# Where the tiles that TensorE reads start in on-chip memory: from 32, 128 or 224 bytes past a multiple of 256 to a multiple of 256

## The chip, the cores and the metric

One core of one Trainium2 chip runs the whole program, in one launch. The metric is the time of that core in microseconds of the device, smaller being better. Of three runs of the kernel before, the median is 2795.87 us (2795.35 to 2801.29).

## The reference

Two layers over 256 context tokens and 2048 latent tokens (a grid of 32 rows by 64 columns), width 1024, all in float32. Cut to what matters here:

```
# layer 0, convolution branch
a, b, z = split(h @ w_in, 3)                # 1024 x 3072
u = depthwise_conv31(a * sigmoid(b)) + dw_b
x = x + gate * ((silu(layer_norm(u)) * silu(z)) @ w_out)
# layer 1, attention branch
q, k, v, z = split(h @ w_in, 4)             # 1024 x 4096, 16 heads of 64
# latent tokens: 8 x 16 grid neighbours (with a bias) and all 512 cached context keys in one softmax
s = concat(q @ k_window + bias, q @ k_context)
p = softmax(s)
o = p_window @ v_window + p_context @ v_context
x = x + gate * ((o * silu(z)) @ w_out)
```

Ahead of each layer stands h = rms_norm(x) * (1 + scale) + shift, with shift, scale and gate from a small product with the conditioning vector; behind the last one stands a final rms_norm.

## The kernel before

Every large product is made of three: each operand is split into a rounded high part and the rest, and high x high, high x low and low x high are added up in one bank of the accumulation memory. The type of these operands is float32r (float32 data that TensorE reads in its reduced-precision form). TensorE issues 16081 matmuls, and nearly each has its own weight load, since the stationary operand changes with every instruction.

Two phases follow each other:

- `phase1`: the convolution layer (`conv_layer`, groups `ci_ps`, an order written out by hand with due times on TensorE, ScalarE, VectorE and GpSimd), its output product (`conv_out_pipeline` and `conv_out`, groups `co_p` and `co_s`), then the projections of the attention layer (`na_rest`, groups `ni_`; `na_values`, groups `v_ps`), with the mixing of context tokens (`pa_`, `po`) and the making of bias tables at their side.
- `phase2`: 64 heads and token groups of four units each. A unit computes scores in `sample_unit` (`sa_S`: 512 context columns and 352 to 480 window columns), softmax probabilities `p`, eight transposes through TensorE (`sa_T`, with the identity as the moving operand), and, for each pair of units, the product with the values (`sa_O`, 256 columns wide). `out_group` multiplies by the output weights (`o`, 512 wide). TensorE and VectorE follow the written order here.

In the projections (`project`) the moving operand is the activation block, 512 or 256 columns wide, and the stationary one the weight:

```
for k in ks:
    matmul(out, wh[:, k, :], hh[:, k, :], ...)   # stationary, moving
    matmul(out, wh[:, k, :], hl[:, k, :], ...)
    matmul(out, wl[:, k, :], hh[:, k, :], ...)
```

In `conv_out` it is the other way round: the normalised tokens (`yh`, `yl`) are stationary and the weight (`wh`, `wl`) moves.

On-chip memory is given out in pools, one behind the other from the left, and from the right end. A pool starts where the one before it ended, so sizes that are no multiple of 256 bytes shift all that follows. The program's own allocation (a matter of the code, no measurement) places the tiles that TensorE reads like this, in bytes of one partition:

| tiles | pool | start past a multiple of 256 |
|---|---|---|
| identity, all-ones | `consts` (left) | 128 |
| split weights (`wh`, `wl` of `ci`, `ni`, `wv`), normalised tokens (`ln_s_yh`, `ln_s_yl`) | `sp`, tag `t4` (left) | 32 |
| output weights `w2`, tokens `y` of `out_group`, context keys and values of the last five of each eight heads | `ap` (left) | 32 |
| activation blocks `h_s_hi`, `h_s_lo`, output weights `co_h`, `co_l` | `slots` (left, behind `sm`) | 224 |
| `h_p_hl`, `h_s_hl`, `ln_y`, context tokens' tiles (`pa_`, `po_`) | right side and `hp` | 224 |
| queries, keys, values, probabilities `p`, `pt`, context keys and values of the first three of each eight heads | `ep`, `pt` (right) | 224 |

So in `ci`, `ni` and `co_s` the moving tile starts at 224 and the stationary one at 32; in `v_ps` it is the other way round (the weight moves, at 32). In `co_p`, `pa_`, `po` and `o` both start alike (224 and 224, or 32 and 32).

Of the kernel before, what the change touches and what calls it, by code (L numbers as in the profile page):

```python
# [11 lines left out]
F32 = mybir.dt.float32  # L12
# [6 lines left out]
P = 128  # L19
# [56 lines left out]
class Kern:  # L76
    def __init__(self, ctx, tc, io):
        self.tc, self.nc, self.io = tc, tc.nc, io
        self.ctx = ctx
        self.more, self.more_bufs, self.turn = None, 0, 0  # L80
        self.tail = False
        self.s0, self.begun = None, []
        self.cp = ctx.enter_context(tc.tile_pool(name="consts", bufs=1))
        self.dr = ctx.enter_context(tc.tile_pool(name="scratch", bufs=1, space=bass.MemoryType.DRAM))
        d = lambda name, shape: self.dr.tile(shape, F32, name=name, tag=name)
        self.zc_d = d("zc_d", [D, NTOK])
        self.wl_d = d("wl_d", [3 * NK, P, D])
        self.vc_d = d("vc_d", [2, D, VCOLS // 2])
        self.x1_d = d("x1_d", [NTOK, D])
        self.qh_d = d("qh_d", [D, NTOK])  # L90
        self.ql_d = d("ql_d", [D, NTOK])
        self.ks_d = d("ks_d", [NH, 2, DH, NTOK])
        self.vp_d = d("vp_d", [NPR, NH, 2, DH])
        self.vs_d = d("vs_d", [GW // CW, NSA // GW, CW, NH, 2, DH])
        self.bm_d = d("bm_d", [NH, 3, P, 3, 480])
        self.zn_d = d("zn_d", [D, NTOK])
        self.kc_d = d("kc_d", [NH, 2, DH, NCTX])
        self.cvs_d = d("cvs_d", [NCTX, NH, 2, DH])
        self.w2_d = d("w2_d", [2, D, D])
        self.x2_d = d("x2_d", [NTOK, D])  # L100
        self.gate_d = d("gate_d", [2, 2, D])
        self.rpb_d = d("rpb_d", [P + 1, RPB_PITCH])
        self.yp_d = d("yp_d", [NK, 2, P, NPR])
# [32 lines left out]
        return t0 if src == "p" else NPR + t0  # L136


    def constants(self):
        nc, cp, io = self.nc, self.cp, self.io  # L140
        self.ident = cp.tile([P, P], F32, tag="ident", name="ident")
        make_identity(nc, self.ident)
        self.ones = cp.tile([P, P], F32, tag="ones", name="ones")
        nc.vector.memset(self.ones, 1.0 / D)
        self.mhalf = cp.tile([P, 1], F32, tag="mhalf", name="mhalf")
        nc.vector.memset(self.mhalf, -0.5)

        c = self.vectors("cond", [io["c_ctx"], io["c"][0]], lambda rows: nc.scalar.activation(rows, rows, AF.Silu))()
        self.cs = cp.tile([P, NK, 32], F32, tag="cs", name="cs")
        nc.vector.memset(self.cs, 0.0)  # L150
        nc.vector.tensor_copy(self.cs[:, :, 0:2], c.rearrange("p g k -> p k g"))
        self.sel = cp.tile([P, 2], F32, tag="sel", name="sel")
        nc.vector.tensor_reduce(out=self.sel, in_=self.ident.rearrange("p (j x) -> p x j", x=32)[:, 0:2], axis=AX.X, op=ALU.add)
# [1218 lines left out]
    def phase1(self):  # L1372
        tc = self.tc
        with ExitStack() as c:
            late = c.enter_context(ExitStack())
            self.rp = late.enter_context(tc.tile_pool(name="rp", bufs=1, side="right"))
            self.sp = Tagged(c.enter_context(tc.tile_pool(name="sp", bufs=1)), {"slot": 4, "t4": 8, "raw": 2, "st": 6})
            self.sm = c.enter_context(tc.tile_pool(name="sm", bufs=3))
            self.sp.apart["slot"] = c.enter_context(tc.tile_pool(name="slots", bufs=1))
            self.ps = c.enter_context(tc.tile_pool(name="ps", bufs=2, space=bass.MemoryType.PSUM))  # L1380
            with tc.tile_pool(name="convp", bufs=2) as self.up, tc.tile_pool(name="acc", bufs=2, space=bass.MemoryType.PSUM) as self.pc:
# [28 lines left out]
            with tc.tile_pool(name="bp", bufs=1, side="right") as self.bp:  # L1410
                with tc.tile_pool(name="mb", bufs=1, side="right") as self.mb, tc.tile_pool(name="more", bufs=1, space=bass.MemoryType.PSUM) as self.more:
                    self.more_bufs = 4
                    side = itertools.chain(self.context_keys(), self.masked_bias())
# [5 lines left out]
                with tc.tile_pool(name="pq", bufs=2, side="right") as pq, tc.tile_pool(name="pqs", bufs=1, space=bass.MemoryType.PSUM) as pps:  # L1419
                    side = itertools.chain(self.gated_weights(), self.context_values())  # L1420
                    side = self.mixed(self.prompt_attention(pq, pps), side, 24 / 52)
# [6 lines left out]
            with tc.tile_pool(name="po", bufs=1, side="right") as po, tc.tile_pool(name="pops", bufs=1, space=bass.MemoryType.PSUM) as pps:  # L1428
                side = self.prompt_out(po, pps)
# [40 lines left out]
    def T(self, tag, shape, dt, name):  # L1470
        if tag in self.early:
            return self.ep.tile(shape, dt, tag=tag, name=name, bufs=self.early[tag])
        return self.sp.tile(shape, dt, tag=tag, name=name)

    def phase2(self):
        tc = self.tc
        with ExitStack() as c:
            bufs = {"w2": 4, "ckr": 8 - NEAR, "cvr": 8 - NEAR, "pt": 2, "st": 4, "y": 14, "x": 3, "row": 1}
            self.sp = Tagged(c.enter_context(tc.tile_pool(name="ap", bufs=1)), bufs)
            self.sm = c.enter_context(tc.tile_pool(name="asm", bufs=6))  # L1480
            self.ps = c.enter_context(tc.tile_pool(name="aps", bufs=1, space=bass.MemoryType.PSUM))
            self.fg = None

            self.sp.apart["pt"] = c.enter_context(tc.tile_pool(name="pt", bufs=1, side="right"))
            E = mybir.EngineType
            c.enter_context(tc.manual_schedule(engines={E.PE, E.DVE}))
            self.attention()
# [138 lines left out]
    def sample_unit(self, hd, j):  # L1626

        nc, T, h, b, G = self.nc, self.T, hd.h, hd.b, hd.G
        nm = f"sa{G}_{h}_{j}"
        R = KEY_ROWS[G][1]  # L1630
        nl = 32 * R
        cs = slice(j * P, j * P + P)
        S = self.bank("S", nm + "_S", 2, 1024)
        jj = j % 2
        ctx, loc = S[:, :512], S[:, 512 : 512 + nl]
        kw = hd.k[:, :, CW * JFIRST[j] : CW * JFIRST[j] + 32].rearrange("p r (a c) -> p a r c", c=CW)
        self.scores(ctx, hd.q[:, cs], hd.ql[:, cs], hd.ctx[h, 0])
        self.scores(loc, hd.q[:, cs], hd.ql[:, cs], kw)
        yield
        m = self.sm.tile([P, 8], F32, tag="m", name=nm + "_m")  # L1640
        nc.vector.tensor_reduce(out=m[:, 0:1], in_=ctx, axis=AX.X, op=ALU.min)  # L1641
        bm = hd.bm[:, JKIND[j], :nl]
        nc.vector.tensor_tensor_reduce(loc, loc, bm, 1.0, m[:, 0:1], ALU.add, ALU.min, accum_out=m[:, 2:3])  # L1643
        yield
        p = T("p", [P, 1024], F32, nm + "_p")
        n = slice(0, 512 + nl)
        nc.scalar.activation(p[:, n], S[:, n], AF.Exp, scale=-1.0, bias=m[:, 2:3], accum_out=m[:, 3:4])  # L1647
        nc.vector.reciprocal(m[:, 3:4], m[:, 3:4])  # L1648
        nc.gpsimd.tensor_scalar(out=p[:, n], in0=p[:, n], scalar1=m[:, 3:4], scalar2=1.0, op0=ALU.mult, op1=ALU.mult)  # L1649
        yield  # L1650
        ts = []
        for part, w, x in ((0, P, 0), (1, CW * R, 512)):
            t = self.bank("T", f"{nm}_T{part}", 2)
            for c in range(4):
                nc.tensor.transpose(t[:w, c * P : c * P + P], p[:, x + c * w : x + c * w + w], self.ident)  # L1655
            ts.append((part, w, t[:w].rearrange("p (c q) -> p c q", c=4)))
        yield
        if jj == 0:
            hd.pt[j // 2] = T("pt", [P, 2, 2, 4, 2, P], F32R, nm + "_pt")
        pt = hd.pt[j // 2]  # L1660
        for part, w, t in ts:

            at = 1 - jj if part == 0 else jj
            nc.scalar.copy(pt[:w, 0, part, :, at], t)  # L1664
            self.rest_dve(pt[:w, 1, part, :, at], t, pt[:w, 0, part, :, at])
# [263 lines left out]
```

## Time and profile before

| | |
|---|---|
| median of three runs | 2795.87 us |
| the profiled execution | 2797.14 us, its span 2795.4 us |
| TensorE busy | 2696.5 us, 96% of the span, 16081 matmuls |
| VectorE, ScalarE, GpSimd busy | 1767.9, 1377.2, 1404.0 us (63%, 49%, 50%) |
| clock granted to TensorE | 0.991 of full speed |
| moved to and from main memory | 533.86 MB, 191 GB/s over the span |

The busy time of TensorE is a sum over pipelined records whose ends are modelled: a 512-wide matmul is recorded with some 395 ns while the next one starts some 230 ns after it. What one costs is the time from its start to the next one's start, called its step from here on; it is read from the timeline, or, where all run back to back, from the record, which is longer than the step by a fixed amount.

### The profile page before, as it was taken

Reading aid. Unit: us, or ns where it says so; the run is one execution under the profiler, and the core shown is the slowest. Engines: PE = TensorE matmul, PEld = TensorE weight load, DVE = VectorE, ACT = ScalarE, POOL = GpSimd, SP = SyncE. Lnnn points to the kernel's source line nnn. Section 1 sums busy time; section 2 is a strip of 40 time slices with the busy share of each in tenths; the row PEclk is TensorE's granted clock in tenths of the full one; section 3 lists DMA queues with packets and bytes.
Section 4 is the critical chain, followed back from the end, with each engine's and each line's share of the span. In section 5 each row is a group of like instructions: output and inputs, shape, how many; then the busy total and the mean of one; then the engine's idle time right before and its main releaser. Section 6 shows DMA issues by size and latency. Waiting matters only on the chain. (4 is left out here: it accounts for less than half of the span.)

```text
span 2795.4 us, 45265 instructions
## 1 busy us (share of the span) xinstructions
PE 2696.5 (96%) x16081; PEld 2320.7 (83%) x16081; DVE 1767.9 (63%) x3052; ACT 1377.2 (49%) x2437; POOL 1404.0 (50%) x1589
## 2 busy tenths in 40 slices
PE   6999999999999999999999999989999999999998
PEld 4888877776777889899998888878888898888887
DVE  4678778878985610013546533368787787878885
ACT  4446454456453322134222244257676676666774
POOL 4686776557554343345223335245455555555563
PEclk9999999999999999999999999999999999999999
DMA  7233554455645554446889986598666767956652
GB/s 258 68 122 121 177 192 123 167 190 193 191 113 164 164 168 129 133 127 193 262 285 330 365 267 183 185 248 229 203 198 197 203 170 204 279 176 202 194 165 100
DMA packets 443833, 533.86 MB, mean 191 GB/s; under 512 B 77745, under 2 KB 320393, under 8 KB 443480
## 3 DMA queue, kind: packets, MB, share of 16 engines
q1 hardware_dynamic: 435568, 503.82, 59.5%
q10 hardware_dynamic: 6664, 22.82, 2.1%
q0 software_dynamic: 1376, 4.33, 0.4%
q8 instruction: 128, 2.10, 0.3%
q14 instruction: 97, 0.79, 0.1%
HBM read 355.14 MB, written 179.79 MB: 191 GB/s over the span
## 5 line engine op out<-in xcount | busy, mean ns | idle before, releaser
L1649 POOL TENSOR_SCALAR sa_p<-sa_p,sa_m 128x992 f32<-128x992 f32 (+2 forms) x256 | 277.6, 1084 | 420.2 <-DVE sa_m L1648 290.0
L514 POOL TENSOR_TENSOR cv_p<-cv_p,cv_p 128x640 f32<-128x640 f32 (+1 forms) x240 | 359.1, 1496 | 123.1 <-ACT cv_p L511 110.1
L1664 ACT CAST sa_pt<-sa_T 128x512 fp32r<-128x512 f32 (+3 forms) x512 | 274.9, 588 | 200.3 <-PE sa_T L1655 195.4
L113 DVE TENSOR_TENSOR sa_pt<-sa_T,sa_pt 128x512 fp32r<-128x512 f32 (+3 forms) x512 | 328.2, 682 | 3.2 <-ACT sa_pt L1664 3.1
L362 PE MATMUL ci_ps<-h_s_hi,ci_wh 128*128 128x512 f32 x768 | 310.7, 405 | 8.2 <-ACT z L481 3.2
L363 PE MATMUL ci_ps<-h_s_lo,ci_wh 128*128 128x512 f32 x768 | 306.8, 399 | 0.0
L364 PE MATMUL ci_ps<-h_s_hi,ci_wl 128*128 128x512 f32 x768 | 306.6, 399 | 0.0
L1647 ACT ACTIVATE sa_p<-sa_S,sa_m 128x992 f32<-128x992 f32 (+2 forms) x256 | 267.0, 1043 | 64.3 <-DVE sa_m L1643 56.5
L1655 PE MATMUL sa_T<-ident,sa_p 128*128 128x128 f32 (+3 forms) x2048 | 271.7, 275 | 9.3 <-DVE sa_pt L113 9.1
L1655 PEld LDWEIGHTS sa_T<-ident,sa_p 128*128 128x128 f32 (+3 forms) x2048 | 236.9, 137 | 46.9 <-issue 14.8
L1641 DVE TENSOR_REDUCE sa_m<-sa_S 128x1 f32<-128x512 f32 x256 | 176.2, 688 | 145.3 <-PE sa_S L1623 134.0
L511 ACT ACTIVATE cv_p<-u,ws 128x640 f32<-128x640 f32 (+1 forms) x256 | 190.8, 777 | 133.8 <-DVE u L478 100.2
L534 DVE SCALAR_TENSOR_TENSOR cv<-u,dw,cv 128x640 f32<-128x640 f32 (+1 forms) x240 | 195.9, 816 | 0.5
L1684 PE MATMUL sa_O<-sa_pt,a_v 120*128 120x256 f32 (+5 forms) x1280 | 191.1, 280 | 0.0
L362 PEld LDWEIGHTS ci_ps<-h_s_hi,ci_wh 128*128 128x128 f32 x768 | 146.3, 191 | 49.9 <-ACT z L481 6.4
L534 DVE SCALAR_TENSOR_TENSOR cv<-cv_d,dw,cv 128x640 f32<-128x640 f32 (+1 forms) x224 | 182.6, 815 | 0.0
L1643 DVE CUSTOM_DVE_ANT_0 sa_S<-sa_S,a_bm,sa_m 128x480 f32<-128x480 f32 (+2 forms) x256 | 170.9, 668 | 13.6 <-DMA a_bm<-bm_d 4.7
L1679 PE MATMUL sa_O<-sa_pt,cv 128*128 128x256 f32 x1024 | 174.8, 293 | 4.7 <-ACT sa_pt L1664 1.1
L364 PEld LDWEIGHTS ci_ps<-h_s_hi,ci_wl 128*128 128x128 f32 x768 | 146.3, 190 | 35.5
L363 PEld LDWEIGHTS ci_ps<-h_s_lo,ci_wh 128*128 128x128 f32 x768 | 146.4, 191 | 32.8
L1684 PEld LDWEIGHTS sa_O<-sa_pt,a_v 120*128 120x128 f32 (+2 forms) x1280 | 166.8, 191 | 0.0
L362 PE MATMUL ni_s<-h_s_hi,nis_wh 128*128 128x512 f32 x384 | 152.6, 397 | 2.3 <-ACT ni_s_f L1047 2.1
(808 smaller groups left out, 7128.8 us busy)
## 6 DMA issues: line engine op xcount, KB each, us to landing
adaw<-in_ada_w SPq DMA_DIRECT2D x24, 1024.0 KB
ci_w<-in_conv_w_in SPq DMA_DIRECT2D x48, 512.0 KB
a_bm<-bm_d SPq DMA_DIRECT2D x32, 720.0 KB
x_s<-in_x_sample SPq DMA_DIRECT2D x32, 512.0 KB
vs_d<-v_s SPq DMA_DIRECT2D x128, 128.0 KB
a_qh<-qh_d SPq DMA_DIRECT2D x128, 128.0 KB
a_ql<-ql_d SPq DMA_DIRECT2D x128, 128.0 KB
a_v<-vs_d SPq DMA_DIRECT2D x32, 480.0 KB
```

The lines of the kernel that those rows point to most:

```text
L113: self.nc.vector.tensor_tensor(out=lo, in0=src, in1=hi.bitcast(F32), op=ALU.subtract)
L362: self.nc.tensor.matmul(out, wh[:, k, :], hh[:, k, :], start=k == 0, stop=False)
L363: self.nc.tensor.matmul(out, wh[:, k, :], hl[:, k, :], start=False, stop=False)
L364: self.nc.tensor.matmul(out, wl[:, k, :], hh[:, k, :], start=False, stop=k == NK - 1)
L511: nc.scalar.activation(t, st["u"][:, 0, j : j + nh], AF.Copy, scale=self.ws[:, ct, j : j + 1])
L514: nc.gpsimd.tensor_tensor(out=st["t", 0], in0=st["t", 0], in1=st["t", j], op=ALU.add)
L534: nc.vector.scalar_tensor_tensor(out=st["acc", b], in0=d, scalar=w, in1=st["acc", b], op0=ALU.mult, op1=ALU.add)
L1647: nc.scalar.activation(p[:, n], S[:, n], AF.Exp, scale=-1.0, bias=m[:, 2:3], accum_out=m[:, 3:4])
L1649: nc.gpsimd.tensor_scalar(out=p[:, n], in0=p[:, n], scalar1=m[:, 3:4], scalar2=1.0, op0=ALU.mult, op1=ALU.mult)
L1655: nc.tensor.transpose(t[:w, c * P : c * P + P], p[:, x + c * w : x + c * w + w], self.ident)
L1664: nc.scalar.copy(pt[:w, 0, part, :, at], t)
L1684: nc.tensor.matmul(dst, v[:w, c0 + c].rearrange("p s d -> p (s d)"), loc[:, lo:hi], start=False, stop=s == 1 and c == 3)
```

## The change

Four paddings are allocated and never touched: 128 bytes ahead of the constants, 224 bytes at the right edge, 96 bytes in a pool of its own behind the constants, and 192 bytes in `sm`. The pool `sm` has three buffers to a tag, so there it is 576 bytes. A fifth, of 128 bytes, stands in `ep` for phase 2. The all-ones tile (512 bytes) moves from the constants into `sm`, which ends with phase 1; it is used only in `norm_stages`. The probabilities `p` become 992 columns wide in place of 1024, which is all that they use (512 + 480); with three buffers, `ep` shrinks by 384 bytes for it and grows by the 128 of padding.

By these sizes all behind the constants on the left moves by 128 - 512 + 96 = -288 bytes (32 past becomes 0), `slots` and what stands behind `sm` by a further 576 + 512 (224 becomes 0), and the right side by -224 (224 becomes 0). No instruction that computes or moves data is added or removed.

```diff
         self.cp = ctx.enter_context(tc.tile_pool(name="consts", bufs=1))
+
+        self.pad(self.cp, 128)
+        self.pad(ctx.enter_context(tc.tile_pool(name="edge", bufs=1, side="right")), 224)
+        self.pad(ctx.enter_context(tc.tile_pool(name="gap", bufs=1)), 96)
...
+    def pad(self, pool, n):
+        pool.tile([P, n // 4], F32, tag="pad", name="pad")
+
     def constants(self):
...
-        self.ones = cp.tile([P, P], F32, tag="ones", name="ones")
+        self.ones = self.sm.tile([P, P], F32, tag="ones", name="ones", bufs=1)
...
             self.sm = c.enter_context(tc.tile_pool(name="sm", bufs=3))
+            self.pad(self.sm, 192)
...
             self.fg = None
+            self.pad(self.ep, 128)
...
-        p = T("p", [P, 1024], F32, nm + "_p")
+        p = T("p", [P, 992], F32, nm + "_p")
```

## The prediction

> **What bounds the kernel now.** I read the page first (busy time, slices), then who made TensorE wait, then busy times by stretch, then TensorE's timeline.
>
> ```profile
> PE 2696.5 (96%) x16081; PEld 2320.7 (83%) x16081; DVE 1767.9 (63%) x3052; ACT 1377.2 (49%) x2437; POOL 1404.0 (50%) x1589
> PEclk9999999999999999999999999999999999999999
> PE ada_ps L227 <- DMA adaw<-in_ada_w: 11.7, 3, 10.8
> PE sa_T L1655 <- DVE sa_pt L113: 9.1, 18, 1.1
> 500.00:720.00 220.00, 212.21 (x958) 161.56 (x957) 184.92 (x248) 123.38 (x183) 138.31 (x113) 0.98 0.55 180
> 2100.00:2400.00 300.00, 296.32 (x2009) 268.32 (x2008) 236.53 (x532) 202.98 (x377) 159.65 (x235) 1.00 0.72 199
> ```
>
> TensorE is busy 96% of the span at full clock, and its two largest waits are 11.7 and 9.1 us in total. In the stretches (length, then busy us of TensorE, its weight loads, VectorE, ScalarE, GpSimd) the next engine, VectorE, has 184.92 of 220 us and 236.53 of 300. So the time is the sum of TensorE's steps (from one matmul's start to the next one's), and the change can act through the step alone. The timeline (start, length of the record, line) gives it; rows between the first and the last of a run are left out:
>
> ```profile
> 300.17 0.40 PE L363 MATMUL ci_ps<-h_s_lo,ci_wh 128*128 128x512 f32 x1
> ...
> 303.90 0.40 PE L364 MATMUL ci_ps<-h_s_hi,ci_wl 128*128 128x512 f32 x1
> ...
> 800.79 0.39 PE L857 MATMUL co_s<-co_h,ln_s_yh 128*128 128x512 f32 x1
> ...
> 801.72 1.09 PE L860 MATMUL co_s<-co_h,ln_s_yl 128*128 128x512 f32 x4
> ...
> 724.67 0.39 PE L857 MATMUL co_p<-co_h,ln_y 128*128 128x512 f32 x1
> ...
> 726.94 0.39 PE L857 MATMUL co_p<-co_h,ln_y 128*128 128x512 f32 x1
> ...
> 2103.13 0.39 PE L1785 MATMUL o<-w2l,1_1_y0h 128*128 128x512 f32 x1
> ...
> 2104.03 0.39 PE L1786 MATMUL o<-w2h,1_1_y0l 128*128 128x512 f32 x1
> ```
>
> All four are 512 columns wide. `ci` makes 16 steps in 303.90 - 300.17 = 3.73 us: 0.233 us each. `co_s` makes 4 in 0.93 us: 0.233. `co_p` makes 10 in 2.27 us: 0.227. `o` makes 4 in 0.90 us: 0.225 to 0.227. `co_s` and `co_p` run the same code lines with the same moving weight; only the stationary tile lies elsewhere. By the allocation, moving and stationary tiles start 224 and 32 bytes past a multiple of 256 in `ci` and `co_s`, but alike in `co_p` (224, 224) and `o` (32, 32). So placing costs something: 6 to 7 ns where the two differ. No row shows a 512-wide step with both at 0.
>
> The 256-wide matmuls:
>
> ```profile
> 1101.07 0.28 PE L362 MATMUL ni_s<-h_s_hl,nip_wh 128*128 128x256 f32 x1
> ...
> 1102.89 0.28 PE L363 MATMUL ni_s<-h_s_hl,nip_wh 128*128 128x256 f32 x1
> ...
> 1334.78 0.28 PE L1011 MATMUL v_ps_s<-wv_s_wh,h_s_lo 128*128 128x256 f32 x1
> ...
> 1335.84 0.28 PE L1011 MATMUL v_ps_s<-wv_s_wh,h_s_lo 128*128 128x256 f32 x1
> ...
> L364 PE MATMUL ni_p<-h_p_hl,nip_wl 128*128 128x256 f32 x192 | 53.2, 277 | 0.0
> L1333 PE MATMUL pa_O<-pa_pt,pa_v x64: 277/283/285, 1663.9 to 1743.8; 128*128 128x256 f32 x64
> ```
>
> `ni` makes 16 steps in 1.82 us (0.114), `v_ps` 9 in 1.06 (0.118); both have tiles that differ (224 and 32, 32 and 224). A 256-wide record is 0.163 us longer than its step (277 against 114 in `ni`), so the median of `pa_O`, 283 ns, is a step of 0.120, with tiles that start alike. At this width equal placing gains nothing by the rows, and may cost.
>
> **The change part by part.** First the sum's main term. The 512-wide matmuls whose two tiles differ now:
>
> ```profile
> L362 PE MATMUL ci_ps<-h_s_hi,ci_wh 128*128 128x512 f32 x768 | 310.7, 405 | 8.2 <-ACT z L481 3.2 <-DVE adao L239 2.3 <-ACT u L476 1.7
> L362 PE MATMUL ni_s<-h_s_hi,nis_wh 128*128 128x512 f32 x384 | 152.6, 397 | 2.3 <-ACT ni_s_f L1047 2.1
> L362 PE MATMUL ni_s<-h_s_hi,nip_wh 128*128 128x512 f32 x192 | 76.4, 398 | 0.0
> L819 PE MATMUL co_s<-co_h,ln_s_yh 128*128 128x512 f32 x160 | 65.5, 409 | 0.8 <-POOL ln_s_yh L107 0.8
> L858 PE MATMUL co_s<-co_l,ln_s_yh 128*128 128x512 f32 x96 | 37.8, 394 | 0.0
> L858 PE MATMUL co_p<-co_l,ln_y 128*128 128x512 f32 x32 | 12.5, 391 | 0.0
> ```
>
> Each row stands for three lines of equal count: 3 x (768 + 384 + 192 + 160 + 96) = 4800. All lie in the first phase, where TensorE issues without waits. With both tiles at 0 they start alike, and I take the step of `co_p`: 0.2333 becomes 0.2267 (two 256-wide `ni` steps of 0.1133 give the same), 6.7 ns x 4800 = **32 us**. The ends: nothing, where 0 and 0 is as bad as 224 and 32; and two further drops of the same 6.7 ns, to 213 ns (the first rival). I take the row that differs in nothing but the placing.
>
> The other 512-wide ones (`o`, `co_p`, `po`, 960; and 512 context scores, which sit between other shapes) count 0: most start alike already.
>
> The 256-wide ones (192 x 3 in `ci`, 192 x 9 in `ni`, as many in `v_ps`, 1792 in `sa_O`, 128 in `pa_`, 5952 in all) count 0 too, between two ends. If all go to the 0.120 of `pa_O`: 6 ns x 1728 in `ni`, 2 ns x 1728 in `v_ps`, 4 ns x 576 in `ci` (whose steps lie between the two), and 1 us for `sa_O` and `pa_`, where about half start alike already: +17 us. The other end comes from products whose moving operand has 2 columns, so that the step is the weight load alone:
>
> ```profile
> 529.16 0.59 PE L243 MATMUL adat_ps<-sel,adam 128*128 128x2 f32 x4
> L243 PE MATMUL adat_ps<-sel,adam x64: 166/251/371, 21.1 to 643.8; 128*128 128x2 f32 x64
> L1321 PE MATMUL pa_T<-ident,pa_p x64: 271/272/274, 1656.0 to 1737.2; 128*128 128x128 f32 x64
> L740 PE MATMUL ln_s_var<-ones,ln_s_s x34: 165/251/374, 664.6 to 977.3; 128*128 128x2 f32 x34
> ...
> 1656.05 1.04 PE L1321 MATMUL pa_T<-ident,pa_p 128*128 128x128 f32 x8
> ```
>
> Four of them span 0.59, less one record of 0.251, over three steps: 0.113. A 256-wide step can't beat that by much: from 0.117, between the two rows, it is 4 ns x (5952 - 1728) = -17 us.
>
> The transposes (some 2500, `sa_T` most) take (1.04 - 0.272) / 7 = 0.110 with the identity at 128 and their data at 224 or 32. That is less than the weight load's 0.113, so I see nothing to win: 0. For the 128 past that some `p` buffers may get at 992 columns, the same 0. `p` itself is read and written in the same 512 + 352 to 480 columns as before: 0. The all-ones tile, now in `sm`, is read for the last time near 977 us (the last row but one), and its pool is given up at the end of the first phase, 800 us later, so nobody waits: 0. The paddings issue nothing on any queue: 0. That DMA or the other engines write faster or slower at the new starts isn't excluded; no row shows it, and they lie beside TensorE: 0, up to the room of VectorE above (15%).
>
> The conditioning tile `cs` lands at 96, not at 0 (its start moves from 224 by 128 - 512); it is the stationary operand of 192 records (`ada_ps`) that the moving weight bounds: 0.
>
> Sum: 2797.1 (the profiled execution) - 32 = 2765; that execution lies 1.3 us over the median, so **2764 us**, 1.1% faster.
>
> **Where the skill bears on it.** The Trainium skill's page "SBUF — State Buffer", section "Who interferes with whom", gives TensorE two read ports of its own, one for the moving operand and one for weight loads, and says that TensorE and ScalarE never wait on anyone; its section "Operand start alignment" asks for no more than a multiple of the element size, and says that its runs timed nothing. By that rule placing would cost nothing and the time would stay at 2796; `co_s` at 0.233 beside `co_p` at 0.227 speaks against it. The skill's page "TensorE: Matmul & The Clock Gate", section "Wait — 56ns, not 53.3ns?", measures a step of N / 2.4 GHz + 2.5 ns in another data type, so 215.8 ns for 512 columns; by it the sum would be -84 us for the 4800 alone, worked out as 17.5 ns each. No row here comes down to it.
>
> **The rivals.**
>
> *Every start off the grid costs, not only unequal ones.* Then `co_p` still pays, and with both at 0 two more drops of 6.7 ns follow: 20 ns x 4800 + 13 ns x 960 = 108 us, and 17 us of the 256-wide ones, 125 in all. Some of it comes back as waits in phase 2, where VectorE and ScalarE follow TensorE closely (`sa_T` waits 18 times for VectorE already), so 105 to 125: **2671 to 2691 us**. For it: the excess is about the same, two such units, in `co_p` and `o` and at both starts 32 and 224, which are alike in being 32 past a multiple of 64. Against it: `pa_O`, where equal placing didn't help at all, and that a cost of each tile by itself would not make `co_s` differ from both `co_p` and `o`.
>
> *Nothing changes.* What sets `co_p` apart could be the distance of whole tiles and not the start within 256. Then 512-wide steps stay at 0.233: **2796 us**. Against it: `o` has other tiles, other distances, and the same 0.227.
>
> *Slower.* If a weight load and a stream that start at the same place meet in the same place at each start, the 256-wide step is that of `pa_O`, 0.120, everywhere. The price is the +17 us above. It decides once the 512-wide ones gain less than 17 / 4800 = 3.5 ns each; if they gain nothing, 2796 + 17 = **2813 us**.
>
> *The change doesn't reach the tiles.* The sizes add up: 128 - 512 + 96 = -288 on the left, + 576 + 512 behind `sm`, -224 on the right; I give it no chance of its own.
>
> **How the numbers follow.** 0.42 for the forecast, 0.27 for every start costing, 0.13 for no change, 0.15 for slower, 0.03 for what I don't see. The forecast by itself spans 2747 to 2781 (256-wide ends -17 and +17). The range 2668 to 2814 takes in all four cases but their far ends. A change within 0.2% (5.6 us) can't be told from none by these runs, whose own spread is 2795.35 to 2801.29. Faster 0.71, same 0.13, slower 0.16.
>
> **What would show it.** In the profile after, `ci`, `ni` and `co_s` records fall from some 395 to 390 ns, 16 steps of `ci` take 3.63 us in place of 3.73, `co_p` and `o` stay at 0.227, and the first scores of phase 2 start about 32 us earlier; phase 2 takes as long as before. If `co_p` and `o` fall too, to 0.213 to 0.220, every start costs. If `ni`'s 256-wide records go from 277 to 283, the slower case is at work. The forecast is wrong if `ci` stays at 0.233, or if VectorE's waits grow by what TensorE saves.

## The result, and the profile after

The changed kernel takes 2773.76 us (median of five, 2771.97 to 2785.73), the kernel before in the same comparison 2800.91 us: ratio 0.9922, 95% interval 0.9903 to 0.9941. The ratio goes over all runs of the comparison; the quotient of the two medians alone is 0.9903. By the ratio that is 0.8% faster, some 22 us (27 by the medians, 20 by the two profiled executions), where 32 were forecast. The measured median lies 10 us over the forecast of 2764, inside the 2747 to 2781 that the forecast gave by itself. The profiled execution took 2777.01 us (span 2775.2, granted clock 0.991, as before). TensorE issues its 16081 matmuls in the same order as before.

The page of the changed kernel: TensorE is busy 14.6 us less; VectorE, ScalarE and GpSimd are within 2.2 us of where they were.

```profile
PE 2681.9 (97%) x16081; PEld 2333.4 (84%) x16081; DVE 1765.7 (64%) x3052; ACT 1377.9 (50%) x2437; POOL 1404.6 (51%) x1589
```

The timeline (start, length of the record, line), against the rows of `ci`, `co_s`, `co_p` and `ni` in the prediction; rows between the first and the last of a run are left out:

```profile
296.19 0.39 PE L370 MATMUL ci_ps<-h_s_lo,ci_wh 128*128 128x512 f32 x1
...
299.82 0.39 PE L371 MATMUL ci_ps<-h_s_hi,ci_wl 128*128 128x512 f32 x1
...
800.00 0.39 PE L864 MATMUL co_s<-co_h,ln_s_yh 128*128 128x512 f32 x1
...
800.91 1.08 PE L867 MATMUL co_s<-co_h,ln_s_yl 128*128 128x512 f32 x4
...
711.35 0.39 PE L864 MATMUL co_p<-co_h,ln_y 128*128 128x512 f32 x1
...
712.71 0.39 PE L864 MATMUL co_p<-co_h,ln_y 128*128 128x512 f32 x1
...
1090.60 0.28 PE L371 MATMUL ni_s<-h_s_hl,nip_wl 128*128 128x256 f32 x1
...
1092.51 0.28 PE L369 MATMUL ni_s<-h_s_hl,nip_wh 128*128 128x256 f32 x1
```

`ci` makes 16 steps in 3.63 us (3.73 before): 0.227. `co_s` makes 4 in 0.91 (0.93). `co_p`, alike before and after, stays at 0.227 (6 in 1.36). But `ni` with 256 columns makes 16 in 1.91 us, 0.119 where it had 0.114 (16 in 1.82). Its group (line, shapes, count, busy us, mean ns of one record) says the same, 277 ns having become 284:

```profile
L371 PE MATMUL ni_p<-h_p_hl,nip_wl 128*128 128x256 f32 x192 | 54.5, 284 | 0.0
```

Two views that the prediction left aside moved as well. First the main transfer queue (packets, MB, time that its packets took as a share of 16 engines' span), the kernel before and then the changed one:

```profile
q1 hardware_dynamic: 435568, 503.82, 59.5%
```

```profile
q1 hardware_dynamic: 435568, 503.82, 57.3%
```

The same packets and bytes, 0.595 x 2795.4 = 1663 us before and 0.573 x 2775.2 = 1590 us after, 4.4% less. Then TensorE's waits for transfers (us in total, times, longest). Before, apart from the 11.7 us that the prediction shows:

```profile
PE sa_S L1622 <- DMA a_k<-ks_d: 3.8, 3, 1.4
PE sa_S L1622 <- DMA a_v<-vs_d: 2.7, 1, 2.7
PE pa_S L1623 <- DMA pa_ql<-ql_d: 1.6, 1, 1.6
PE sa_S L1622 <- DMA a_qh<-qh_d: 1.0, 1, 1.0
PE sa_S L1623 <- DMA a_ql<-ql_d: 0.4, 1, 0.4
PE ck_t L1180 <- DMA ck<-in_cache_k: 0.3, 1, 0.3
```

And all that is left of them after:

```profile
PE ada_ps L234 <- DMA adaw<-in_ada_w: 11.6, 3, 10.6
PE sa_S L1631 <- DMA a_bm<-bm_d: 2.5, 1, 2.5
PE sa_S L1631 <- DMA ck<-kc_d: 1.7, 1, 1.7
```

They sum up to 21.5 us before and 15.8 after; the first of them, the wait for `adaw`, hardly moved (11.7 and 11.6), the others went from 9.8 to 4.2.

From the starts of all matmuls in both traces one can make a full account. I took for each 512-wide step under 246.7 ns what it has over 226.67 (without the 192 of `ada_ps`, which are only 32 columns of the stationary side and follow one another after some 7 ns), and for each 256-wide one under 140 ns what it has over 120 (negative where it is quicker), and put all the rest (longer steps, other shapes, waits) in one sum:

| us | before | after | difference |
|---|---|---|---|
| 512-wide steps, over 226.7 ns each | 36.0 | 9.9 | -26.1 |
| 256-wide steps, over 120 ns each | -19.5 | -2.9 | +16.6 |
| all else | 2765.7 | 2755.3 | -10.4 |
| first to last matmul | 2782.3 | 2762.4 | -19.9 |

So the 512-wide steps gained what was forecast less a fifth, the 256-wide ones gave more than half of it back, and 10 us came from where nothing was expected.

### The profile page after: what moved, and what is told of

The parts are those of the page before. It is cut to its first block, busy times and chain, and to the rows that moved or that the text cites. A ratio compares the mean times of both kernels' runs of the same rounds, so it can differ in the third digit from the quotient of the medians.

```text
span 2775.2 us, 45265 instructions
## 1 busy us (share of the span) xinstructions
PE 2681.9 (97%) x16081; PEld 2333.4 (84%) x16081; DVE 1765.7 (64%) x3052; ACT 1377.9 (50%) x2437; POOL 1404.6 (51%) x1589
## 3 DMA queue, kind: packets, MB, share of 16 engines
q1 hardware_dynamic: 435568, 503.82, 57.3%
## 4 chain that ended last, share of the span: by engine, by line
PE 84%; DVE 6%; DMA 4%; ACT 3%; POOL 2%; issue 2%; SPq 1%; POOLq 0%; DVEq 0%; ACTq 0%
PE sa_T L1664 7%; PE ci_ps L369 6%; PE ci_ps L370 6%; PE ci_ps L371 6%; PE ni_s L369 6%; PE ni_s L370 6%; PE ni_s L371 6%; PE sa_O L1693 5%; PE sa_O L1688 4%; PE sa_S L1632 4%; PE sa_S L1631 4%; PE o L1793 2%; PE o L1795 2%; PE o L1794 2%; PE v_ps_s L1016 2%; PE v_ps_s L1018 2%
## 5 line engine op out<-in xcount | busy, mean ns | idle before, releaser
L1664 PE MATMUL sa_T<-ident,sa_p 128*128 128x128 f32 (+3 forms) x2048 | 270.4, 274 | 10.4 <-DVE sa_pt L117 10.3
```

## The experiments

The theory of the steps (R): TensorE's step depends on where the moving and the stationary tile start relative to each other within 256 bytes, and not on the grid. Its rival (G): each start off the grid costs by itself. For the 10 us a second theory (D) came up with the first results: transfers into and out of tiles that start on the grid take less time.

**Strings of matmuls (`micro`).** One mover and one stationary tile, read at chosen offsets:

```diff
+        for i in range(steps):
+            a = s // 4 + P * (i % 16)
+            b = m // 4 + 512 * ((i // 2) % 4)
+            nc.tensor.matmul(pm[:, :n], sta[:, a : a + P], mov[:, b : b + n], start=i == 0, stop=i == steps - 1)
```

> Leaves the whole computation out: strings of 64 float32r matmuls back to back, each with its own 128-column weight load, 512, 256 and 384 columns wide, with the moving and the stationary tile started at chosen bytes past a multiple of 256 (0, 16, 32, 64, 96, 128, 160, 192, 224): one shifted against the other, both shifted alike, and the pairs 224/32 and 32/224 of the kernel before. Theory R (what counts is where the two tiles start relative to each other, not where on the 256 grid): at 512 columns the step is 226.7 ns whenever both start alike, also at 32 and at 224, and 233.3 ns for 224/32 and for 64 apart; at 256 columns 120 ns when alike and 113 to 118 ns when 64 apart, and some other offsets between 107 and 120. Rival G (each tile off the multiple of 256 costs by itself): both at 32 or both at 224 is slower than both at 0 by 3 to 7 ns at 512, and one tile shifted costs half of what two shifted cost. Rival K (the steps of the kernel come from its order of tiles and banks, not from placing): all offsets give the same step within 1 ns at each width.

The groups of its trace, with the mean record in ns behind the busy time. `wide` is 512 columns, `half` 256; `m` and `s` name the start of the moving and the stationary tile, a, c, d, h and i being 0, 32, 64, 192 and 224:

```profile
L110 PE MATMUL wide_mi_sc<-mov,sta 128*128 128x512 f32 x64 | 15.1, 395 | 0.0
L110 PE MATMUL wide_mh_sa<-mov,sta 128*128 128x512 f32 x64 | 15.1, 396 | 0.0
L110 PE MATMUL wide_md_sa<-mov,sta 128*128 128x512 f32 x64 | 14.8, 391 | 0.0
L110 PE MATMUL wide_mi_si<-mov,sta 128*128 128x512 f32 x64 | 14.7, 389 | 0.0
L110 PE MATMUL wide_ma_sa<-mov,sta 128*128 128x512 f32 x64 | 14.7, 389 | 0.0
L110 PE MATMUL half_ma_sa<-mov,sta 128*128 128x256 f32 x64 | 7.8, 283 | 0.0
L110 PE MATMUL half_mi_si<-mov,sta 128*128 128x256 f32 x64 | 7.8, 283 | 0.0
L110 PE MATMUL half_mi_sc<-mov,sta 128*128 128x256 f32 x64 | 7.7, 281 | 0.0
L110 PE MATMUL half_md_sa<-mov,sta 128*128 128x256 f32 x64 | 7.4, 276 | 0.0
```

The mean steps, from the starts: alike, 226.7 to 227.4 ns at 512 columns, 173.5 to 173.8 at 384 and 119.8 to 120.0 at 256, at every common start that is a multiple of 32 (at 16, where the kernel has no tile, 230.0 and 118.3). Unlike, 228.9 to 234.3 ns at 512 and 113.4 to 120.0 at 256; the moving tile 64 ahead is mildest at 512 (228.9 to 229.2). R stands, and G and K fall: 224 and 224 is as quick as 0 and 0 within 0.4 ns, and unlike starts differ from alike ones by up to 7.6. R had 233.3 ns for all starts 64 apart, too much where the moving tile is ahead. The 256-wide steps were expected at 113 to 118 when 64 apart, and so they came; but 224 against 32 gave 117.8 here, and 0.114 in `ni` of the kernel before. The strings by themselves say the same: with the moving tile 64 ahead, 64 against 0 took 113.4 ns, but 0 against 192 and 32 against 224, the same offset within 256, took 117.8. So with unlike starts the offset alone does not fix the 256-wide step.

**The rest of the change alone (`rest_only`).** The kernel before, with the narrower `p` and the moved tile, all tiles of the large products left at the same starts past a multiple of 256:

```diff
-        self.ones = cp.tile([P, P], F32, tag="ones", name="ones")
+        self.ones = self.sm.tile([P, P], F32, tag="ones", name="ones", bufs=1)
...
+            self.pad(self.ep, 128)
...
-        p = T("p", [P, 1024], F32, nm + "_p")
+        p = T("p", [P, 992], F32, nm + "_p")
```

> The kernel before with the probabilities 992 columns wide, the 128 bytes of padding in their pool and the all-ones tile moved to the first phase's pool, which together leave every tile of the large products where it was. Theory R: no difference, ratio 0.999 to 1.001. Rival S (a part of the gain comes from the smaller probabilities or the moved tile): ratio 0.994 to 0.998.

Measured: ratio 0.9998 (0.9987 to 1.0009). These parts are worth nothing by themselves.

**Everything alike, but off the grid (`alike224`, then `alike64`).** The changed kernel with another amount of padding, here for `alike224` (`alike64` has 192 in `cp` and 160 at the edge):

```diff
-        self.pad(self.cp, 128)
-        self.pad(ctx.enter_context(tc.tile_pool(name="edge", bufs=1, side="right")), 224)
+        self.pad(self.cp, 352)
```

> The changed kernel with every tile that TensorE reads 224 bytes past a multiple of 256 instead of at 0: nothing starts on the grid, but moving and stationary tile start alike everywhere. Theory R (relative start counts): the same as the changed kernel, ratio to the kernel before 0.992 (0.990 to 0.994), some 2774 us; the 512-wide steps of ci, ni and co_s 226.7 ns, the 256-wide of ni 120 ns. Rival G (each start off the grid costs by itself): no gain or a loss, ratio 1.000 to 1.007, 512-wide steps at 233 ns or more.

Measured: 0.9963 (0.9950 to 0.9976), between the two. The steps are those of the changed kernel (10.1 and -2.9 us in the account above), so R is right about them. But all else is 2766.9 us, as in the kernel before, and so is the queue:

```profile
q1 hardware_dynamic: 435568, 503.82, 59.9%
```

Half of the gain was missing, and it was not in TensorE's steps. This is where D came from. The next runs went with the changed kernel on one chip.

> The changed kernel, unedited, as the yardstick beside its variants on one chip. Theory C (the gain of alike224 was smaller only because of the chip it ran on): ratio to before about 0.996 here as well. Theory R+D (the relative start sets TensorE's steps; besides, transfers into tiles that start on a coarse grid take less time, 57.3% of the queues' time against 59.5 to 59.9%, which takes some 10 us of waits away): ratio 0.991 to 0.993, with the main queue at 57.3%.

Measured: 0.9927 (0.9908 to 0.9946), queue 57.4%: the chip was not the cause.

> The changed kernel with every tile that TensorE reads, and every tile that transfers fill, 64 bytes further, so that all start alike at 64 past a multiple of 256. Theory R: TensorE's back-to-back steps as in the changed kernel (226.7 ns at 512 columns, 120 at 256). Theory D64 (transfers need starts at a multiple of 64 bytes): main queue at 57.3%, time as the changed kernel within 0.15%. Rival D256 (they need a multiple of 256): main queue near 59.9%, ratio to before 0.995 to 0.998, as alike224. Rival N (alike224's extra waits were chance): no difference in waits, and no link with the queue's share.

Measured: 0.9968 (0.9955 to 0.9982). Steps again as in the changed kernel (9.9 and -2.9), all else 2770.7. Its queue and its largest waits for transfers:

```profile
q1 hardware_dynamic: 435568, 503.82, 59.3%
```

```profile
PE ada_ps L234 <- DMA adaw<-in_ada_w: 12.1, 2, 11.4
PE sa_S L1631 <- DMA ck<-kc_d: 5.5, 1, 5.5
PE sa_S L1631 <- DMA a_k<-ks_d: 3.7, 3, 1.6
```

A multiple of 64 does not do; D256 stands, D64 and N fall.

**The counterpart: on the grid, but unlike (`t4_off`).**

```diff
+            self.pad(c.enter_context(tc.tile_pool(name="t4gap", bufs=1)), 64)
+            self.sp.apart["t4"] = c.enter_context(tc.tile_pool(name="t4", bufs=1))
             self.sm = c.enter_context(tc.tile_pool(name="sm", bufs=3))
-            self.pad(self.sm, 192)
+            self.pad(self.sm, 256)
```

> The changed kernel with only the t4 buffers (split weights, normalised tokens) 64 bytes further: in the first phase moving and stationary tile are 64 bytes apart as in the kernel before (0 and 64 for 224 and 32 before that minus 32 and 224 modulo 256), while nearly all transfers still go into tiles at a multiple of 256. The counterpart of alike224, which has equal starts off the grid. Theory R+D (TensorE's steps follow the relative start, waits on transfers follow the absolute start, and the two add up): steps as before in ci, ni, co_s (233 ns at 512, 113 to 118 at 256), that is 9 to 11 us above the changed kernel, waits and the main queue's share (57.4 to 58%) as in the changed kernel; ratio to before 0.995 to 0.998. Rival R (all of the gain is the relative start): ratio 0.999 to 1.001. Rival D (all of it is the transfers): ratio 0.992 to 0.993.

Measured: 0.9956 (0.9939 to 0.9972). The 512-wide steps are those of the kernel before (35.7 us in the account), the 256-wide ones come most of the way back to them (-14.7, where the kernel before has -19.5), and the queue is that of the changed kernel:

```profile
L370 PE MATMUL ci_ps<-h_s_lo,ci_wh 128*128 128x512 f32 x768 | 305.3, 398 | 0.0
```

```profile
q1 hardware_dynamic: 435568, 503.82, 57.2%
```

In the changed kernel the mean of that group is 394, in the kernel before 399. The two halves add up: equal starts off the grid give 0.32 to 0.37%, the grid with unequal starts 0.44%, together 0.76 to 0.81%, and the change gave 0.73 to 0.78%, where each of these figures has an interval of 0.13 to 0.19 points to either side.

**Transfers by themselves (`dma`).** 16 transfers of 512 KB to a group:

```diff
+        return big[j % 8][:, o // 4 : o // 4 + 1024]     # o: start past a multiple of 256
```

> Leaves the whole computation out: only transfers of 512 KB, 16 to a group, one group after the other, into and out of tiles that start 0, 32, 64, 128, 192 or 224 bytes past a multiple of 256, in runs of 512, 2048 and 4096 bytes of one partition (in) and 4096 and 512 bytes (out). Theory D: groups at 0 are the quickest, by 3 to 10%, at least where the runs are short; D256: 64 and 128 are as slow as 32 and 224; D64: 64, 128 and 192 are as quick as 0. Rival N: all starts within 1%, the difference in the queue's share of the kernels has another cause.

The timeline of VectorE, which touches a buffer after two outgoing transfers of 512-byte runs have read it: the group at start 0, and then the group at 64:

```profile
579.83 0.96 DVE L123 MEMSET big<- 128x1088 f32 x1 [2.06 <-DMA cols_d<-big]
...
601.01 0.96 DVE L123 MEMSET big<- 128x1088 f32 x1 [2.07 <-DMA cols_d<-big]
...
632.48 0.96 DVE L123 MEMSET big<- 128x1088 f32 x1 [2.74 <-DMA cols_d<-big]
...
654.81 0.96 DVE L123 MEMSET big<- 128x1088 f32 x1 [2.79 <-DMA cols_d<-big]
```

At 0, seven such touches take 21.18 us: 3.03 for two transfers. At 64, six take 22.33: 3.72. From such gaps of all groups, where they have settled, us for one transfer of 512 KB:

| runs | start 0 | 32, 64, 128, 192, 224 |
|---|---|---|
| in, 512 bytes | 1.51 | 1.81 |
| in, 2048 bytes | 1.28 | 1.36 |
| in, 4096 bytes | 1.24 | 1.28 |
| out, 512 bytes | 1.51 | 1.86 |
| out, 4096 bytes | 1.25 | 1.25 to 1.30 |

(The first group, in with 512 bytes at 0, is not settled: its gaps run from under 0.1 to 2.75, and 1.51 is the middle one; the clean 1.51 is that of the outgoing group. In the next, in with 512 bytes at 32, the first seven gaps are over 4 us, and 1.81 is that of the eight behind them.) D256 holds, and how far a start is off makes no difference to the short runs. Incoming, the price is one fixed amount for each run: 0.30 us for the 1024 runs of 512 bytes in a transfer, 0.074 for the 256 of 2048, 0.041 for the 128 of 4096, which is 0.29 to 0.32 ns for each. As an estimate for the kernel, 0.3 ns for each of the queue's 435568 packets would be some 130 us; its time fell by 73 us (1663 to 1590), so the price is large enough to account for it, if about half of the packets paid it. The Trainium skill states the rule on its page "DMA: Bandwidth & Descriptors", section "How a descriptor splits into AXI transactions": a transaction must start at a 256-byte boundary, so a run of whole 256-byte pieces that starts off it needs one more. The incoming runs agree with that count, one more price for each run, and so do the short outgoing ones; the outgoing ones of 4096 bytes show nothing at 32, 64 and 128. The runs do not follow the beats in the section's table: by an estimate counted in its way, a 512-byte run from 32 would fetch 17 beats and one from 224 would fetch 23, and both took the same, 1.81 us coming in and 1.85 going out.

**Apart only where it helps (`shift64`, `mixed`, `mixed2`).** Equal starts are right at 512 columns and wrong at 256, so a better placing than the change's should exist. First, the slots and the right side 64 bytes further:

```diff
+            self.pad(c.enter_context(tc.tile_pool(name="gap2", bufs=1)), 64)
             self.sp.apart["slot"] = c.enter_context(tc.tile_pool(name="slots", bufs=1))
```

(and 160 in place of 224 at the edge).

> The changed kernel with the activation blocks (slots) and the whole right side 64 bytes further, weights left at 0: moving and stationary tile 64 bytes apart in the projections, everything still at a multiple of 64. Theory R, with the steps of the strings (moving tile 64 ahead: 228.9 ns at 512 columns, 113.4 at 256; stationary tile 64 ahead: 117.8 at 256): 512-wide projections +2.2 ns on 4032 steps, +9 us; the stationary weights of co_s likewise +2 us; 256-wide -6.4 ns on 2304 and -2.2 on 1728, -18 us; so 4 to 10 us below the changed kernel. Rival (placing as in the kernel before, 224 against 32, is what any unlike placing gives: 233.3 ns): 512-wide +27 us, 256-wide -16, so 8 to 14 us above the changed kernel. Under D64 the main queue stays at 57.3%.

Measured: 0.9933 (0.9911 to 0.9955), no gain on the changed kernel. The steps did what R said (512-wide +8.2 us, 256-wide -13.8, together -5.6), but these tiles receive transfers: queue 58.9%, all else 2769.2, and the gain was gone. So only tiles that no transfer fills may be moved:

```diff
             self.hp = c.enter_context(tc.tile_pool(name="hp", bufs=1))
+            self.pad(self.hp, 64)
...
+            self.pad(c.enter_context(tc.tile_pool(name="ptgap", bufs=1, side="right")), 64)
             self.sp.apart["pt"] = c.enter_context(tc.tile_pool(name="pt", bufs=1, side="right"))
```

> The changed kernel with only the tiles of 256-wide products set apart: the shared 256-token block of the attention projections 64 bytes further (moving in 1152 steps of ni, stationary in 384 of v_ps) and the transposed probabilities pt 64 bytes back (moving in 1792 steps of sa_O at 256 columns); the 512-wide products keep equal starts. Theory R: ni -6.5 ns on 1152 steps, v_ps -2 on 384, sa_O up to -5.5 on 1792: 8 to 18 us below the changed kernel, ratio to before 0.985 to 0.989, the fastest of all. Rival W (phase 2 is set by the chain between the engines and not by sa_O's steps): only ni's and v_ps's part comes, 8 us or less. Rival: no gain, the 256-wide steps stay at 120 ns.

Measured: 0.9915 (0.9894 to 0.9936), too near to 0.9927 to tell. `ni` went to 118 ns and not to 113, and a third of its 256-wide steps lie in another block that was not moved: -5.1 us in the 256-wide account instead of 8 to 18. The last one moves that block too (a view 48 elements into a wider slot) and keeps what lies behind `hp` on the grid:

```diff
-                both = self.slot(F32R, f"{name}_hl", [P, 2, NK, n], late)
+                e = 0 if late else 48
+                w = self.slot(F32R, f"{name}_hl", [P, 2 * NK * n + (64 if e else 0)], late)
+                both = w[:, e : e + 2 * NK * n].rearrange("p (s k n) -> p s k n", s=2, k=NK)
...
+            self.pad(self.hp, 192)
+            self.pad(c.enter_context(tc.tile_pool(name="gap3", bufs=1)), 64)
```

(`pt` as in `mixed`; 64 bytes ahead of `sm` take the place of the 192 in it, for room.)

> The changed kernel with all blocks of 256 tokens 192 bytes past the grid (in the slots of the right side and in hp; moving in 2304 steps of ni and ci, stationary in 576 of v_ps), the pair 192 and 0 standing as 224 and 32 did in the kernel before, and the transposed probabilities pt at 192 as in mixed; what transfers fill stays on the grid, also behind hp, where mixed had moved it. Theory R: ni 113 ns instead of 120 on 1728 steps, -11 us; ci 117, -1.5; v_ps -1; sa_O -2: 12 to 16 us below the changed kernel, ratio to before 0.986 to 0.989. Rival M (which step a string of unlike tiles takes is not fixed by the offset alone: mixed took 118 where the strings gave 113): 118 ns, 5 to 7 us below, ratio 0.990 to 0.991.

Measured: 2769.64 us, 0.9880 (0.9863 to 0.9898). It is the fastest of all, and its interval ends below those of the changed kernel's two comparisons (not below that of `mixed`). One of its 256-wide groups:

```profile
L373 PE MATMUL ni_p<-h_p_hl,nip_wl 128*128 128x256 f32 x192 | 53.9, 281 | 0.0
```

281 ns is a step of 118, not of 113 (277): rival M was right about the step, while ratio and sum came out as R had them. The account gives 7.5 us at 512 and -13.3 at 256, 12.8 below the changed kernel. But R's largest term, 11 us from `ni` at 256 columns, came to 5; `sa_O` (2 us) and `ci` (1) came about as expected, and the rest is `v_ps` (2.4, where R had 1) and the 512-wide steps (2.4, where R had nothing). That R's total was met is therefore chance in part.

All of them in one table (us as in the account above, of one execution of each kernel):

| kernel | starts | transfers' tiles | 512 | 256 | all else | queue | waits for transfers | ratio |
|---|---|---|---|---|---|---|---|---|
| before | unlike | off | 36.0 | -19.5 | 2765.7 | 59.5% | 21.5 | 1 |
| rest_only | unlike | off | 35.9 | -19.5 | 2763.7 | 59.7% | 21.6 | 0.9998 |
| alike224 | alike | off | 10.1 | -2.9 | 2766.9 | 59.9% | 21.0 | 0.9963 |
| alike64 | alike | off | 9.9 | -2.9 | 2770.7 | 59.3% | 24.9 | 0.9968 |
| shift64 | unlike | partly off | 18.1 | -16.7 | 2769.2 | 58.9% | 17.7 | 0.9933 |
| t4_off | unlike | on | 35.7 | -14.7 | 2745.8 | 57.2% | 14.4 | 0.9956 |
| after | alike | on | 9.9 | -2.9 | 2755.3 | 57.3% | 15.8 | 0.9922 |
| after_b | alike | on | 9.8 | -3.0 | 2753.3 | 57.4% | 13.7 | 0.9927 |
| mixed | 512 alike, some 256 not | mostly on | 9.5 | -8.0 | 2757.0 | 57.4% | 13.7 | 0.9915 |
| mixed2 | 512 alike, most 256 not | on | 7.5 | -13.3 | 2762.7 | 57.6% | 19.2 | 0.9880 |

All else varies by several us from one execution to the next, and the profiled execution lies up to 7 us from the median of its kernel's runs. Moved by that distance, all else is 2769 to 2770 us in the four kernels with the transfers' tiles off the grid, 2766 in `shift64`, and 2752 to 2761 in the five with them on it or mostly so. `mixed2` is the highest of these five, with the longest waits for transfers; why is open.

## Why the prediction was right, and where its sum was off

The direction and the main mechanism were right. Its steps, in order:

- *TensorE's steps set the time, and unequal starts cost the 512-wide ones 6.7 ns*: right. `rest_only`, `alike224` and `t4_off` show that the relative start, and nothing else in the change, moves these steps. The term was 32 us and came to some 26: of the 4800 steps some are not at the settled value, in any of the kernels, and 191 take more than 246.7 ns in the kernel before, so that they stand in all else. In the changed kernel 1916 of the 2304 steps of `ci` lie within 1.5 ns of 226.7, 1440 of 1728 in `ni`, but only 416 of 768 in `co_s`. What holds the others above it was not found.
- *256-wide steps, counted 0 between +17 and -17*: this is the step that failed. They came to +16.6, the upper end. The row that told it was in the prediction: `pa_O`, the one 256-wide row shown there whose tiles start alike throughout, at 0.120 beside `ni` at 0.114. The middle was taken where one end had a row for just this case and the other only a bound from another shape. The strings show that alike is 120 at any common start that is a multiple of 32.
- *Transfers, counted 0 because they lie beside TensorE*: wrong by about 10 us in the other direction. The text named that they might be written faster at the new starts, and priced it by VectorE's room. But 21.5 us of TensorE's waits were waits for transfers, all of them in views that were at hand, 9.8 of them behind the one at the start, and they were a part that could shrink. What the runs show is that the grid shortens transfers (`dma`), that the queue's share follows it in all kernels, and that all else falls with it, as do the waits for transfers in all but `mixed2` (19.2 us). Not every microsecond of all else has been traced to its transfer: 5.7 of the 10.4 us are waits that the profile names so; that the rest hangs on transfers too is argued from the kernels on and off the grid, and not shown wait by wait.
- *Every start off the grid costs (first rival)*: refuted for TensorE, by `co_p` at 0.227 before and after, by 224/224 in the strings and by `alike224`. It is true of transfers, which that rival did not speak of.
- *Nothing changes*, and *slower*: the first is refuted; the second had the right step (0.120 nearly everywhere) and the right price, and lost because the 512-wide steps gained some 26.1 / 4800 = 5.4 ns, more than the 3.5 from which it decides. Its reason, that a weight load and a stream meet in the same place, was not tested.
- *The first scores some 32 us earlier, phase 2 as long as before*: wrong in both halves.

```profile
L1622 PE MATMUL sa_S<-ck,a_qh x2: 389/430/470, 1824.8 to 1831.3; 128*128 128x512 f32 x2
```

```profile
L1631 PE MATMUL sa_S<-ck,a_qh x2: 389/431/473, 1812.9 to 1819.4; 128*128 128x512 f32 x2
```

They start 11.9 us earlier (1824.8 before, 1812.9 after), since the first phase also holds nearly all the 256-wide losses, and phase 2 is 8.3 us shorter (970.6 before and 962.3 after, up to the end of the span), since most of the fall of all else lies there. Of these 8.3 us, 4.8 are waits of the scores for transfers of keys, values and queries (6.5 behind the first score before, 1.7 after).

The transposes, the conditioning tile and the paddings counted 0: the other shapes show no shift that stands out of the variation of all else, and `rest_only` bears it out for `p` and the all-ones tile.

That the sum came within 10 us is luck in part. Two terms counted as nothing missed by 16.6 and 10.4 us, and in opposite directions. By the steps alone the change is worth 9.5 us (-26.1 and +16.6), less than a third of the 32 that were forecast for them, and that is what `alike224` and `alike64` measured (0.37 and 0.32%).

## What to carry to other kernels

Look at the start addresses of tiles as a parameter: for float32r products with a weight load to each matmul, which is all that was measured here, TensorE wants the two tiles of a wide (512) product at equal starts within 256 bytes and those of a 256-wide one at unequal starts (of which some are no better than equal ones), and a tile that transfers fill or empty in short runs wants a multiple of 256. The two effects are separate, so they can be had together, as in `mixed2`: pad what transfers touch to the grid, and shift only tiles that engines write. Before a shorter transfer is priced at nothing, add up how long the bounding engine waits for transfers now.

## What the runs showed of the hardware

- With equal starts that are a multiple of 32, a float32r step with its own 128-column weight load takes 120.0 ns at 256 columns, 173.5 at 384 and 226.7 at 512: a straight line with 0.417 ns for each column and 13.3 ns on top. With unequal starts (multiples of 32) 512 columns take 228.9 to 234.3 ns and 256 columns 113.4 to 120.0.
- The same unequal pair can give several steps: at 256 columns, 224 against 32 took 117.8 ns in the strings, and in the kernel before a median of 117 in `ci` and 113 in `ni`; 192 against 0 took 113.5 in the strings and 117 to 118 in `ni` of `mixed2`. What decides between them is open; it was not tried.
- A transfer in runs of 512 bytes takes 20 to 23% longer where its tile starts off a multiple of 256, whether by 32 or by 224; in runs of 4096 bytes 3% inward, and up to 4% outward, at 192 and 224 alone.
